# Layer-1 input projections by a seven-product block scheme, with the layer-1 memory keys and values computed in layer 0

## The chip, the cores and the metric

The kernel is one program on all 8 cores of a Trainium2 chip; every core works on 1024 of the 8192 tokens. The metric is the device time of the slowest core, in microseconds (us).

A program on all cores has two states. In the fast one, executions of a kernel agree within about 0.3%. In the slow one, the cores of one die (cores 0 to 3, or 4 to 7), sometimes of both, are granted a lower TensorE clock, and the time is longer. Every run lists span and clock of each core, so the state is known.

The engines are called as the profile calls them: PE (matmul), PEld (weight load), DVE (vector), ACT (scalar), POOL and SP (here they mostly issue transfers).

## The reference, cut to what matters

A decoder trunk of two layers, width 2048. Layer 0 mixes tokens by dilated attention, layer 1 by a gated unit; both also attend to 256 memory tokens; each is followed by a SwiGLU block of width 5632.

```python
def _spatial_gating_mixer(h, w_in, ln_g, ln_b, w_spatial, b_spatial):   # layer 1
    proj = h @ w_in                               # 2048 -> u 1536, v 1536, q_mem 512
    u, v, q_mem = jnp.split(proj, [SGU_W, 2 * SGU_W], axis=-1)
    u = jax.nn.gelu(u)
    v = _layer_norm(jax.nn.gelu(v), ln_g, ln_b)
    v = v.reshape(b, s // SGU_CHUNK, SGU_CHUNK, SGU_GROUPS, SGU_GROUP_DIM)
    ...                                           # w_s: masked lower triangular, 128 x 128 per group
    mixed = jnp.einsum('gts,bnsgc->bntgc', w_s, v) + b_spatial.T[None, None, :, :, None]
    return u * mixed.reshape(b, s, SGU_W), q_mem

def _memory_attention(q_mem, mem_n, w_mem_kv):    # both layers
    kv = mem_n @ w_mem_kv                         # depends on mem and weights only, not on x
    ...
```

Two facts carry the change. `h @ w_in` is a large matrix product, which a two-by-two block scheme (Strassen's, in Winograd's form) computes with seven block products for eight, at the price of sums of blocks. And the memory keys and values of layer 1 do not depend on `x`, so they can be computed at any time.

## The kernel before

The feed-forward blocks of both layers already use the seven-product scheme (`quads` forms the token sums, `tsum` the weight sums, the `prod` calls are the seven products). Layer 1's input projections do not: each output tile is 16 products over the contraction of 2048.

Weights come as 1 MB bf16 or f16 blocks (2 MB of f32 in HBM, cast by the transfer), through a ring of four slots. A load waits until the previous user of its slot is done.

```python
    class Ring:
        order = (96, 104, 112, 120)
        def load(self, src, half=False, at=None):
            if at is None:
                at = self.order[self.n % 4]
                self.n += 1
            ...
            pooldma(lambda g: g.dma_start(out=rb.ap, in_=src), [], [rb.r()], f"w{at}", 2.1)

    # layer 0: values and keys, query/key of head set 0, memory k/v of layer 0, memory queries
    for f in v_ + qk0[0:4] + k_ + qk0[4:8] + mu[0:4] + qk0[8:12] + mu[4:6] + qm_units():
        f()
    ...
    # layer 1 (after the feed-forward of layer 0)
    for th in range(2):
        for m in range(4):
            q_unit(m, th, wq[m // 2])        # memory queries
    l1_mem_b()                               # memory k/v of layer 1: 4 weight blocks
    for th in range(2):
        for m in range(4):
            ...
            mem_attn(1, m, ...)
    l1_tables()
    v_all((0, 1))                            # v, gelu, layer norm per tile
    for pc in range(6):
        u_piece(pc, "u")                     # u, gelu, then the gate of v and the product with u
```

In `v_all` the tokens are the stationary operand (512 weight columns stream past), in `u_piece` and `q_unit` the weights are (512 tokens stream past). An operation line of the profile such as L974 or L1180 is the line of a helper, so one line stands for many operations.

The softmax here doesn't subtract the row's maximum and nothing guards it: scores larger than these inputs give would overflow.

## Time and profile before

| | |
|---|---|
| three runs | 2665.65, 2873.76, 3029.14 us |
| profiled execution | 2664.8 us, clocks 0.987 to 0.989 on all cores |
| PE busy | 96% of the span |
| layer-1 projections and gating | 260 us, of which PE busy 248 |
| four matmul groups there | v 384, u 384, query 128 products of 512 columns; memory k/v 64 of 256 and 32 of 512 |

The head of the profile page gives busy time of each engine, share of the span, and count of instructions; part 4 gives the chain of waits that ended last, by engine.

```profile
PE 2559.5 (96%) x12625; PEld 1209.1 (45%) x12703; DVE 1379.7 (52%) x2321; ACT 721.2 (27%) x1139; POOL 146.5 (5%) x247
PE 86%; DMA 5%; DVE 4%; issue 3%; ACT 2%; POOL 0%; DVEq 0%; ACTq 0%; another core or an unknown queue 0%; SPq 0%; POOLq 0%
```

PE is the limit nearly everywhere. The next view gives, for a stretch of time, its length, the busy time (and instructions) of each engine, the granted PE clock, the busy share of the DMA engines, and GB/s. This is the kernel before; the first two stretches are layer 0's memory weights, the last two layer 1's projections and, inside them, the memory attention.

```profile
core 2: us, PE busy (x) PEld busy (x) DVE busy (x) ACT busy (x) POOL busy (x), PEclk, DMA share, GB/s
306.80:317.20 10.40, 6.62 (x77) 4.94 (x78) 8.48 (x26) 1.77 (x6) 2.12 (x4) 1.00 0.86 127
317.20:357.30 40.10, 39.53 (x212) 20.95 (x215) 20.82 (x42) 6.76 (x13) 2.11 (x4) 1.00 0.94 154
1462.00:1722.00 260.00, 248.14 (x1337) 121.03 (x1339) 107.05 (x225) 81.28 (x125) 10.77 (x20) 1.00 0.47 90
1528.60:1567.00 38.40, 31.96 (x142) 13.46 (x144) 12.04 (x21) 31.85 (x47) 0.00 (x0) 1.00 0.07 21
```

In layer 0 the DMA engines are 0.86 to 0.94 busy. In layer 1 they are half idle. In the memory attention PE idles 6.4 of 38.4 us while ACT is busy 31.9.

The timeline of PE shows how layer 0's memory queries (L747) follow layer 0's memory values (L713) without a gap. Columns: start, length, engine, line, operation, output<-inputs, shape, count.

```profile
353.89 1.89 PE L713 MATMUL psall<-ring_0_137,stg_54 128*128 128x512 bf16 x8
355.62 1.89 PE L713 MATMUL psall<-ring_0_136,stg_54 128*128 128x512 bf16 x8
357.34 1.89 PE L747 MATMUL psall<-hT,ring_0_138 128*128 128x512 bf16 x8
359.07 1.89 PE L713 MATMUL psall<-ring_0_137,stg_54 128*128 128x512 bf16 x7
360.80 10.52 PE L747 MATMUL psall<-hT,ring_0_138 128*128 128x512 bf16 x47
```

Where PE waits in layer 1, longest in total first: total us, times, longest.

```profile
PE psall L1474 <- ACT vtm_a L1480: 2.8, 2, 1.8
PE psall L1426 <- DVE Btab L1430: 1.7, 1, 1.7
PE psall L1538 <- DVE hTq L1044: 1.6, 1, 1.6
PE psall L1501 <- DVE vtm_b L1493: 1.6, 1, 1.6
```

L1474 is v waiting for a gelu (the table of ACT alternates between gelu and exp there), L1501 is the gate waiting for the layer norm.

### The profile page before, as it was taken

To read this page: it belongs to the slowest core of one execution; us is meant where nothing else is said; L and a number is where in the kernel's file an instruction comes from. 1 tells how busy PE (TensorE), PEld (TensorE's weight loads), DVE (VectorE), ACT (ScalarE), POOL (GpSimd) and SP (SyncE) were. 2 spreads that over 40 slices of the span, in tenths; PEclk is the share of its full clock that TensorE was granted. 3 is DMA by queue.
4 is the path that set the end of the run, shared out by engine and by line. 5 is a ranking of instruction groups with operands and counts; after the bars stand their busy time and mean duration, and the time that the engine had idled before them with its cause. 6 is when DMAs were issued, how large, how long until landed. Compare 5 with 4: busy or idle time off the path is not lost.

```text
span 2664.8 us, 34291 instructions; the slowest of 8 cores (2648.5 to 2664.8 us)
## 1 busy us (share of the span) xinstructions
PE 2559.5 (96%) x12625; PEld 1209.1 (45%) x12703; DVE 1379.7 (52%) x2321; ACT 721.2 (27%) x1139; POOL 146.5 (5%) x247
## 2 busy tenths in 40 slices
PE   6999999999999999989999999999999999999998
PEld 2344446554444444444444534445444444444443
DVE  4873536657434343446766425327444434356766
ACT  3532224235323232320002351115322323210003
POOL 2001000000000000000000000000000000000002
PEclk9999999999999999999999999999999999999999
DMA  9745772343565656566662814432656555566654
GB/s 153 105 61 93 127 131 49 64 121 92 109 115 117 116 103 116 101 144 127 141 135 50 166 33 86 88 64 49 130 107 126 106 113 105 111 138 132 137 124 143
DMA packets 91892, 288.30 MB, mean 108 GB/s; under 512 B 6736, under 2 KB 56656, under 8 KB 68304
## 3 DMA queue, kind: packets, MB, share of 16 engines
q0 software_dynamic: 36912, 217.87, 47.0%
q1 hardware_dynamic: 54816, 68.24, 8.0%
q8 instruction: 103, 1.69, 0.3%
q14 instruction: 61, 0.50, 0.1%
HBM read 471.44 MB, written 32.51 MB: 189 GB/s over the span
## 4 chain that ended last, share of the span: by engine, by line
PE 86%; DMA 5%; DVE 4%; issue 3%; ACT 2%; POOL 0%; DVEq 0%; ACTq 0%; another core or an unknown queue 0%; SPq 0%; POOLq 0%
PE psall L1180 38%; PE psall L1327 17%; PE psall L729 6%; PE psall L1561 4%; PE psall L1523 3%; PE psall L684 2%; PE psall L639 2%; PE psall L1474 2%; PE psall L655 2%; PE psall L1073 2%; DMA hid<-fs_74 1%; PE psall L1538 1%; PE psall L747 1%; PE psall L883 1%; PE psall L1038 1%
## 5 line engine op out<-in xcount | busy, mean ns | idle before, releaser
L974 DVE TENSOR_TENSOR xs<-psall,xs 128x512 f32<-128x512 f32 x400 | 269.4, 690 | 233.1 <-PE psall L1327 156.7
L1180 PE MATMUL psall<-hTq,ft_71 128*128 128x512 f16 x704 | 167.9, 382 | 3.7 <-DVE hTq L1063 3.7
L1180 PE MATMUL psall<-hTq,ft_72 128*128 128x512 f16 x704 | 166.3, 379 | 0.0
L1180 PEld LDWEIGHTS psall<-hTq,ft_71 128*128 128x128 f16 x704 | 69.1, 98 | 88.1 <-issue 6.3
L1180 PEld LDWEIGHTS psall<-hTq,ft_72 128*128 128x128 f16 x704 | 68.9, 98 | 83.1
L1180 PE MATMUL psall<-hTq,fr_67 128*128 128x512 f16 x384 | 87.3, 379 | 1.0 <-DVE hTq L1044 1.0
L980 ACT ACTIVATE junkB_127<-xs 128x1024 bf16<-128x1024 f32 x16 | 16.8, 1051 | 246.9 <-DVE xs L974 246.4
L1180 PE MATMUL psall<-Sq_65,ft_71 128*128 128x512 f16 x352 | 83.3, 379 | 0.0
L1180 PE MATMUL psall<-Sq_64,ft_72 128*128 128x512 f16 x352 | 83.2, 379 | 0.0
L1180 PE MATMUL psall<-Sq_65,ft_72 128*128 128x512 f16 x352 | 83.2, 379 | 0.0
L1180 PE MATMUL psall<-Sq_64,ft_71 128*128 128x512 f16 x352 | 83.2, 379 | 0.0
L1180 PE MATMUL psall<-hTq,fr_70 128*128 128x512 f16 x352 | 79.9, 379 | 0.0
L1180 PE MATMUL psall<-hTq,fr_69 128*128 128x512 f16 x352 | 79.7, 379 | 0.0
L1180 PE MATMUL psall<-hTq,fr_68 128*128 128x512 f16 x320 | 72.7, 379 | 0.0
L980 ACT ACTIVATE junkB_126<-xs 128x1024 bf16<-128x1024 f32 x8 | 8.5, 1057 | 234.3 <-DVE xs L974 233.7
L1161 DVE TENSOR_TENSOR ft_71<-fr_67 128x2048 f16<-128x2048 f16 x22 | 26.9, 1225 | 84.3 <-PE psall L1180 83.9
L1161 DVE TENSOR_TENSOR ft_72<-fr_70 128x2048 f16<-128x2048 f16 x20 | 24.5, 1225 | 83.2 <-PE psall L1180 83.2
L1044 DVE TENSOR_TENSOR hTq<-psall,gT_s 128x1024 f16<-128x1024 f16 x48 | 56.9, 1218 | 19.2 <-PE psall L1038 18.8
L1161 DVE TENSOR_TENSOR ft_72<-fr_68 128x2048 f16<-128x2048 f16 x20 | 24.5, 1225 | 81.5 <-PE psall L1180 79.4
L1161 DVE TENSOR_TENSOR ft_71<-fr_69 128x2048 f16<-128x2048 f16 x20 | 24.5, 1225 | 80.8 <-PE psall L1180 80.8
L1186 ACT COPY snap_79<-psall 128x512 f32<-128x512 f32 x59 | 34.6, 586 | 113.8 <-PE psall L1180 113.8
L1186 ACT COPY snap_81<-psall 128x512 f32<-128x512 f32 x59 | 34.6, 586 | 112.9 <-PE psall L1180 112.9
(1321 smaller groups left out, 4762.4 us busy)
## 6 DMA issues: line engine op xcount, KB each, us to landing
fr_67<-wgu POOLq DMA_DIRECT2D x24, 1024.0 KB, 8.6
fr_69<-wgu POOLq DMA_DIRECT2D x22, 1024.0 KB, 8.5
fr_70<-wgu POOLq DMA_DIRECT2D x22, 1024.0 KB, 8.5
fr_68<-wgu POOLq DMA_DIRECT2D x20, 1024.0 KB, 8.6
ring_0_135<-w POOLq DMA_DIRECT2D x8, 1024.0 KB, 9.7
xs<-xo SPq DMA_DIRECT2D x8, 1024.0 KB, 10.4
y<-xs SPq DMA_DIRECT2D x16, 512.0 KB, 4.1
ring_0_136<-w POOLq DMA_DIRECT2D x7, 1024.0 KB, 11.6
```

Of the source, the lines that this page charges most:

```text
L639: pe([(lambda t, k=k, w=w: t.matmul(bank(b), hb[k * n + tt * 128:k * n + tt * 128 + 128], w[(k % 8) * 512:(k % 8 + 1) * 512], start=(k == ...
L655: pe([(lambda t, k=k: t.matmul(bank(b)[:, 0:n], w[k * 256 + c0:k * 256 + c0 + 128], hb[k * n:(k + 1) * n], start=(k == 0), stop=(k == 15)) ...
L684: pe([(lambda t, k=k, hf=hf: t.matmul(bank(b), own_tile(hT[k * TOK:(k + 1) * TOK], gi, j), ws[hf][(k % 8) * 512:(k % 8 + 1) * 512], start= ...
L729: proj(b, 512, [(lambda t, k=k: t.matmul(bank(b), w[k * 256 + c * 128:k * 256 + c * 128 + 128], hT[k * TOK + th * 512:k * TOK + th * 512 + ...
L974: dve(lambda v: v.tensor_tensor(out=xa, in0=bank(b), in1=xa, op=ALU.add), [PB(b), xr], [xr], 512)
L1044: dve(lambda v, b=b, gb=gb, dst=dst: v.tensor_tensor(out=dst, in0=bankb(b).rearrange("p (a c) -> p a c", c=128), in1=gb, op=ALU.mult), [PB ...
L1161: dve(lambda v: v.tensor_tensor(out=T[0:2048], in0=w[1024:3072], in1=w[0:2048], op=ALU.subtract), [w.r(0, 3072)], [T.r(0, 2048)], 2048, 2)
L1180: pe([(lambda t, k=k: t.matmul(bank(b), W[blk * 1024 + k * 128:blk * 1024 + k * 128 + 128], f(k), start=(first and k == 0), stop=(last and ...
L1186: act(lambda a: a.copy(out=s_.ap, in_=bank(b)), [PB(b)], [s_.r()], 512)
L1327: pe([(lambda t, k=k: t.matmul(bank(b), f(u, k), w[k * 512:(k + 1) * 512], start=(first and k == 0), stop=(last and k == hG - 1), skip_gro ...
L1523: proj(b, 512, [(lambda t, k=k, b=b, c=c, th=th, w=w: t.matmul(bank(b), w[k * 256 + c * 128:k * 256 + c * 128 + 128], hTq[hq_(k, th * 512, ...
L1561: pe([(lambda t_, k=k, hh=hh, hf=hf: t_.matmul(bank(b), gTm[(hh * 8 + k) * TOK + t * 128:(hh * 8 + k) * TOK + t * 128 + 128], ws[hh][k * 5 ...
```

## The change

The intent: take 7/8 of the PE work of three projections (v, u, memory queries), keep the products that go into the gate in one buffer (v, then the gated v, then u times it, all in place), and move the layer-1 memory keys and values out of layer 1, whose buffers the new sums need, into layer 0. The core of the diff, with cuts:

```diff
-    memd = nc.dram_tensor("memd", [128, 4096], BF16).ap()
+    mk1d = nc.dram_tensor("mk1d", [128, 1024], F16).ap()
+    mv1d = nc.dram_tensor("mv1d", [128, 1024], BF16).ap()
 ...
-    spdma(lambda q: q.dma_start(out=memd, in_=memT1p.ap), [memT1p.r()], [kreg("memd")], "m1", 1.05)
 ...
-    for f in v_ + qk0[0:4] + k_ + qk0[4:8] + mu[0:4] + qk0[8:12] + mu[4:6] + qm_units():
+    mu1 = mem_units(1, memT1p, mkt, mvt)
+    for f in v_ + qk0[0:4] + k_ + qk0[4:8] + mu[0:4] + qk0[8:12] + mu[4:6] + mu1:
         f()
+    spdma(lambda q: q.dma_start(out=mk1d, in_=mkt.ap), ...)
+    spdma(lambda q: q.dma_start(out=mv1d, in_=mvt.ap), ...)
+    for f in qm_units():
+        f()
 ... layer 1, v: two token tiles and 256 columns to a product, seven products for a block of 4 tiles x 512 columns
+        def f1():
+            prod(X, A(0, 0), "B11", True, False)
+            st["s1"] = snapshot(X)
+        def f2():
+            prod(Y, A(1, 0), "B21", True, True)
+            add(fin(0, 0), two(bank(Y)), [PB(Y)], st["s1"])
+        def f3():
+            prod(X, S(1), "T2", False, False)
+            st["s2"] = snapshot(X)
 ...
+    v_units(0)
+    quads(0)
+    quads(1)
+    sums_v(vu[0][0])
+    v_raw(0)
 ... layer 1, query and u pieces, seven products each; memory attention between them
+    tsum_u(wq0)
+    piece_u(wq0, (12, 13), False)
+    tsum_u(wq1)
+    mem_pair((0, 1))
+    piece_u(wq1, (14, 15), False)
+    ln_all()
+    mem_pair((2, 3))
+    l1_tables()
+    for pc in range(6):
+        for c in range(2):
+            for th in range(2):
+                gate(2 * pc + c, th)
+        tsum_u(wu[pc])
+        piece_u(wu[pc], (2 * pc, 2 * pc + 1), True)
 ...
+            act(lambda a: a.activation(out=u.ap, in_=src, func=AF.Gelu), ..., after=[mem_last[0]])
```

A `snapshot` is a copy of a running partial sum out of PSUM by ACT: the scheme reuses partial sums in several outputs.

## The prediction

> All numbers are for the fast state: the profiled execution (2664.8 us, all clocks 0.987 to 0.989) matches the fastest time (2665.65). 2873.76 and 3029.14 I take for the slow state.
>
> **What bounds it now.** Busy table: PE 96%, DVE 52%, ACT 27%; the chain of waits is 86% PE. By windows, layer-1 projections and gating (1462 to 1722 us) take 260 us with PE busy 248: 12 us idle, 6.4 of it in the memory attention (1528 to 1567), 1.6 before a gate (layer norm). At 306 to 357 us (layer 0's memory weights) the DMA engines are 0.86 to 0.96 busy and PE waits 3.6 us for a weight block: already DMA-bound.
>
> **Removed.** Timeline: eight 128x512 matmuls take 1.726 us (0.216 each), 32 of 128x256 take 3.49 us (0.109 each, own weight load each, so loads stay hidden). Before: v 384, u 384, query 128 of 512 columns = 193.3 us. After: v 672 of 256 columns (73.2), u and query 448 of 512 (96.6) = 169.8. PE saves 23.5 us, all on the chain. The normed memory's store, just ahead of the DMA-bound stretch, goes: about 2 us.
>
> **Added.** DVE: token sums 16 x 0.68, v weight sums 12 x 1.225, u and query weight sums 8 x 2.6: 46 us. ACT: some 56 snapshots of 0.59 = 33 us. Per 12 us piece ACT is busy about 5 us, DVE 9 to 10: hidden, as in the feed-forward, which runs the same scheme without gaps. At the entry (1462 to 1500) DVE is 27.5 of 38 us busy and gets 10 us more before the third product can run, and gelu and exp tables (1.28 us a load) may alternate: I charge 3 us. Layer norm is batched behind the query pieces; gelu is held until memory attention is done, so the gelu/exp swaps there go: 5 us less idle, limited by single accumulator banks.
>
> **Moved.** Layer-1 memory k/v (13.9 us of PE, 1514.7 to 1528.6) goes to layer 0, ahead of the memory queries. PE work is neutral, but its four 1 MB blocks enter, at about 339 us, a queue that delivers one in 7 to 8 us, while each feeds PE 3.5 us. The four-slot ring puts the query block behind them: it lands at 383 to 390 us instead of 355.6, with 14 us of work to cover 26 to 32. Nothing else is ready (later units share PSUM banks in program order). I charge 12 us (8 to 18) of new PE wait. The Trainium skill ("Trainium Kernel Development and Optimization", Key Constraints) says that DMAs of all queues share 16 engines and interleave; landing times growing from 8.5 to 18 us in this stretch agree.
>
> **Sum.** 2665 - 23.5 - 2 + 3 - 5 + 12 = about 2650 us. 8 in 10: 2636 to 2668. Faster by over 2%: 2%; within 2%: 96%; slower by over 2%: 2%.
>
> **What would show it.** 896 matmuls of 512 columns become 448 plus 672 of 256; the stretch from 1462 to 1722 shrinks by 13.9 + 23.5 + a few us; in layer 0, a new DMA-ended wait of 8 to 18 us before the memory-query matmuls, whose end moves from 387 to about 411 to 416 us.
>
> **What would make it wrong.** No wait in layer 0: about 2638. 256-column products over 0.109 us, DVE lateness in v pieces, or memory attention serialised by one accumulator: up to 2670.

## The result, and the profile after

| | before | changed |
|---|---|---|
| runs | 2665.65, 2873.76, 3029.14, 2664.49 us | 2651.20, 2927.68, 2989.39, 2653.95 us |
| state | fast, slow, slow, fast | fast, slow, slow, fast |
| median of all four | 2769.70 | 2790.81 |
| profiled execution (fast) | 2664.8 | 2649.6 |

The ratio of the fast runs is 0.9954 (95% interval 0.993 to 0.9978). A ratio is the mean time of one kernel's fast runs over that of the other's of the same rounds, so it is not quite the ratio of the medians.

The fast runs, 2651.20 and 2653.95, lie in the predicted range, 1 and 4 us from the predicted 2650. The median of all four runs, 2790.81, is the midpoint between a fast and a slow run and lies far above it. Both things are taken up below.

The head of the page and the chain by engine, changed kernel:

```profile
PE 2547.4 (96%) x12927; PEld 1230.0 (46%) x12927; DVE 1424.3 (54%) x2341; ACT 747.5 (28%) x1191; POOL 146.8 (6%) x248
PE 87%; DMA 6%; DVE 3%; issue 2%; ACT 1%; POOL 0%; DVEq 0%; ACTq 0%; POOLq 0%; SPq 0%
```

PE work fell by 12 us; DVE and ACT work rose by 45 and 26 us and mostly hid. DMA's rounded share of the chain went from 5% to 6%; what stands behind it, PE's timeline in layer 0 shows. Changed kernel; L717 and L729 are now memory keys and values, of layer 0 (input `stg`) and then of layer 1 (`memT1p`), L763 the memory queries. The brackets give the idle time before a group and what ended it.

```profile
358.09 1.91 PE L717 MATMUL psall<-memT1p,ring_0_148 128*128 128x256 bf16 x16
359.84 1.89 PE L729 MATMUL psall<-ring_0_147,stg_56 128*128 128x512 bf16 x8
361.57 1.91 PE L717 MATMUL psall<-memT1p,ring_0_148 128*128 128x256 bf16 x16
365.14 3.65 PE L717 MATMUL psall<-memT1p,ring_0_145 128*128 128x256 bf16 x32 [1.66 <-DMA ring_0_145<-wkv]
372.08 6.36 PE L729 MATMUL psall<-ring_0_146,memT1p 128*128 128x512 bf16 x16 [3.29 <-DMA ring_0_146<-wkv]
378.93 3.61 PE L729 MATMUL psall<-ring_0_147,memT1p 128*128 128x512 bf16 x16 [0.49 <-DMA ring_0_147<-wkv]
386.18 13.97 PE L763 MATMUL psall<-hT,ring_0_148 128*128 128x512 bf16 x64 [3.64 <-DMA ring_0_148<-w]
```

Four waits, 9.1 us in all, each ended by a weight block. And one group is slow: at 372.08, 16 products take 6.36 us where the same 16 take 3.61 us at 378.93, since PE ran at half clock then (the clock records of this core have 0.5 from 370.8 us on, for 6.8 us). Queries start at 386.2, not at 357.3.

In layer 1 the changed kernel's waits of PE are others than before:

```profile
PE psall L1718 <- DVE G_93 L1721: 1.9, 5, 0.8
PE psall L1513 <- DVE tV_99 L1485: 1.5, 1, 1.5
PE psall L1767 <- DVE G_93 L1697: 1.4, 1, 1.4
PE psall L1513 <- DVE G_93 L1541: 1.0, 1, 1.0
PE psall L1718 <- DVE Btab L1738: 0.7, 1, 0.7
PE psall L1734 <- DVE Btab L1738: 0.7, 1, 0.7
```

and by stretches (all of layer 1's projections; the memory attention; the first gates):

```profile
core 1: us, PE busy (x) PEld busy (x) DVE busy (x) ACT busy (x) POOL busy (x), PEclk, DMA share, GB/s
1475.00:1709.00 234.00, 225.12 (x1518) 136.23 (x1517) 156.08 (x250) 111.14 (x182) 10.92 (x20) 1.00 0.46 82
1597.00:1640.00 43.00, 43.00 (x201) 19.47 (x200) 18.44 (x29) 24.64 (x45) 1.41 (x2) 1.00 0.32 68
1640.00:1656.00 16.00, 11.93 (x78) 5.72 (x77) 15.18 (x33) 7.30 (x13) 1.06 (x2) 1.00 0.51 89
```

The memory attention, 6.4 us idle before, runs with PE busy 43.00 of 43.00. Right behind it is a new hole: in 16 us of gate tables and first gates PE idles 4.1 us, with DVE busy 15.2 of 16.

To see where time came from, I took marks from the trace of all eight cores (first or last matmul of a stage) and averaged over the cores. In us; positive means that the kernel reaches the mark later than the kernel before.

| mark | changed | control (changed, run again) |
|---|---|---|
| end of layer 0's halo keys | -1.5 | -1.3 |
| end of the memory queries, layer 0 | +25.4 | +25.8 |
| last gate/up product of layer 0 | +24.8 | +24.7 |
| last down product of layer 0 | +20.4 | +21.7 |
| first output-projection product of layer 1 | -13.8 | -12.6 |
| end | -15.9 | -14.2 |

So layer 0 loses 27 us up to the end of the queries, of which 13.9 are the matmuls that moved, and layer 1 wins 34. The down-projection of layer 0 gets 3.0 to 4.4 us shorter. Of this, 2.6 us are the change's too: layer 1's first products already run there, 25 query products of 512 columns before (5.4 us), 26 v products of 256 columns after (2.8 us). The rest differs from run to run. Behind the first output-projection product the changed kernel is 1.6 to 2.1 us shorter; so are all its versions below (1.6 to 3.8), while e2, a version of the kernel before, is not (0.4 longer). Nothing here explains that part.

### The profile page after: what moved, and what is told of

Its sections match the earlier page's. It is cut to its first block, busy times and chain, and to the rows that moved or that the text cites. A ratio compares the mean times of both kernels' runs of the same rounds, so it can differ in the third digit from the quotient of the medians.

```text
span 2649.6 us, 34898 instructions; the slowest of 8 cores (2634.0 to 2649.6 us)
## 1 busy us (share of the span) xinstructions
PE 2547.4 (96%) x12927; PEld 1230.0 (46%) x12927; DVE 1424.3 (54%) x2341; ACT 747.5 (28%) x1191; POOL 146.8 (6%) x248
## 4 chain that ended last, share of the span: by engine, by line
PE 87%; DMA 6%; DVE 3%; issue 2%; ACT 1%; POOL 0%; DVEq 0%; ACTq 0%; POOLq 0%; SPq 0%
PE psall L1210 38%; PE psall L1357 17%; PE psall L745 6%; PE psall L1767 4%; PE psall L1673 3%; PE psall L1513 2%; PE psall L671 2%; PE psall L700 2%; PE psall L655 2%; PE psall L1103 2%; DMA stg_56<-xT 1%; PE psall L763 1%; PE psall L913 1%; DMA ring_0_148<-w 1%; PE psall L1068 1%
## 5 line engine op out<-in xcount | busy, mean ns | idle before, releaser
L1191 DVE TENSOR_TENSOR ft_73<-fr_69 128x2048 f16<-128x2048 f16 x22 | 26.9, 1224 | 85.1 <-PE psall L1210 84.2
## 6 DMA issues: line engine op xcount, KB each, us to landing
fr_69<-wgu POOLq DMA_DIRECT2D x24, 1024.0 KB, 10.2
```

The costliest lines, as they stand in the source:

```text
L1191: dve(lambda v: v.tensor_tensor(out=T[0:2048], in0=w[1024:3072], in1=w[0:2048], op=ALU.subtract), [w.r(0, 3072)], [T.r(0, 2048)], 2048, 2)
```

## The experiments

All times below are of fast runs. "Layer-1 stage" is the time from the last down product of layer 0 to the first output-projection product of layer 1, mean over the eight cores of the profiled execution; it is 233.4 us before, and 199.2 and 199.1 in the two profiles of the changed kernel. Job A ran on one chip, job C on another. In job A the kernel before had one run of 2697.24 us that counts as fast; without it its fast runs average 2667.1. It lowers all four ratios of that job by 0.2%, so I compare times and marks. The differences of 9 us are told from noise because the fast runs of a job hardly overlap (control 2650.8 to 2657.5 us, e1 2642.8 to 2647.3, e3 2642.5 to 2645.7).

| run | job | fast runs of it, mean us | fast ratio to before | end of memory queries and k/v, layer 0 | layer-1 stage against before |
|---|---|---|---|---|---|
| kernel before | A, C | 2667.1, 2666.2 | | 0 | 0 |
| control (changed) | A | 2653.1 | 0.9929 | +25.8 | -34.3 |
| e1 no loads | A | 2644.6 | 0.9897 | +15.4 | -34.1 |
| e2 before with loads | A | 2683.1 | 1.0041 | +18.3 | +1.2 |
| e3 between | A | 2644.2 | 0.9895 | +14.3 | -34.1 |
| e4b gates later | C | 2654.7 | 0.9957 | +24.9 | -33.7 |
| e5b both | C | 2644.2 | 0.9917 | +13.6 | -33.8 |
| e6b v by eight | C | 2657.4 | 0.9967 | +25.2 | -29.5 |
| e7b u by eight | C | 2665.9 | 0.9999 | +25.0 | -21.8 |

(In e3 and e5b the memory values come last, not the queries; the figure is the end of whichever is last.)

**Theory.** The products save what their count says; half of that is lost in layer 0, because four more weight blocks stand in the queue ahead of the query weights. **Rival 1**: the loss in layer 0 lies in the moved matmuls themselves, their PSUM banks and evictions, not in the loads. **Rival 2**: the sum of bytes counts, not the order. **Rival 3**: the seven-product pieces fall short of their count, since snapshots, sums and merges hold them up.

### Control: the changed kernel again

> The changed kernel once more, unedited, as a control on the chip of the next runs. Expected: about 0.995 of the kernel before (2651 to 2655 us where that takes 2665), on fast runs, and the same stage lengths as in the first profile: about 25 us later than before at the end of the memory queries, about 34 us shorter from the end of layer 0 to the output projection of layer 1. Rival (the small gain is noise of the run): the two stages differ from the first profile by more than a few us.

Measured: 2653.1 us, marks within 1.7 us of the first profile (table above). The gain of 14 us over 2667.1 and its two parts are real and repeat.

### e1: the same matmuls without the loads

```diff
-    mu1 = mem_units(1, memT1p, mkt, mvt)
+    mu1 = mem_units(1, memT1p, mkt, mvt, reuse=True)   # reads the two blocks of layer 0's memory values
```

> Layer-1 memory k/v in layer 0 keeps its 96 matmuls but reads the two weight blocks of layer 0's memory values, which are already there: the four extra loads are gone, and the result is wrong on purpose. My theory (a queue of weight loads, one block in 7 to 8 us, is what PE waits for): the end of the memory queries moves from 25 us later than before to about 14 us later (the matmuls alone), and the time falls by 9 to 13 us, to about 0.991 of before. Rival (the wait is in the matmuls' own PSUM banks, evictions or order, not in the loads): nothing changes, 0.995.

Measured: the result is wrong (relative error 0.06). 2644.6 us, 8.5 less than the control; the end of the queries comes 15.4 us later than before, where layer 0's halo keys already end 1.5 later: the 13.9 us of the matmuls and nothing more. The stretch of 60 us that holds memory k/v and queries, first the kernel before, then changed, then e1 (each under its own column line):

```profile
core 2: us, PE busy (x) PEld busy (x) DVE busy (x) ACT busy (x) POOL busy (x), PEclk, DMA share, GB/s
355.00:415.00 60.00, 59.68 (x278) 27.46 (x283) 20.00 (x37) 26.71 (x50) 2.77 (x6) 1.00 0.56 94
```

```profile
core 1: us, PE busy (x) PEld busy (x) DVE busy (x) ACT busy (x) POOL busy (x), PEclk, DMA share, GB/s
355.00:415.00 60.00, 50.92 (x254) 25.02 (x252) 4.35 (x8) 9.37 (x18) 4.72 (x9) 0.94 0.87 149
```

```profile
core 0: us, PE busy (x) PEld busy (x) DVE busy (x) ACT busy (x) POOL busy (x), PEclk, DMA share, GB/s
355.00:415.00 60.00, 59.69 (x305) 30.31 (x310) 10.18 (x20) 17.80 (x35) 2.64 (x5) 1.00 0.52 99
```

With the loads PE idles 9 us and is granted 0.94 of its clock, at a DMA share of 0.87; without them it is busy throughout at full clock, at 0.52. Rival 1 falls.

### e2: the kernel before, with the loads and nothing else

```diff
-    ... + mu[4:6] + qm_units():
+    ... + mu[4:6] + [lambda i=i: R.load(wkv[4 + i]) for i in range(4)] + qm_units():
```

> The kernel before, plus only the four extra weight loads of layer-1 memory k/v at the same place in the ring of layer 0; nothing reads them, so the result stays right. My theory: the loads alone delay the memory queries by as much as the changed kernel does, since the matmuls there hide under the loads: end of the memory queries 22 to 28 us later, time 1.008 to 1.011 of before (2687 to 2694 us). Rival (the matmuls are what costs): no delay, or only a few us, 1.000.

Measured: 2683.1 us, 16 more than before; the queries end 18.3 us later and layer 0's attention 15.6 us later. The direction is as expected, so four loads that nobody reads cost more than the whole change saves. The size is under the range that I had written (22 to 28; 2687 to 2694). The timeline of the POOL queue gives the likely reason: with no matmul holding the slots, it issued the first query block ahead of the last two idle blocks (at 357.94, against 360.88 and 362.60), so two blocks fewer stood before it than in the changed kernel; it landed at 373.1 us, there at 385.8. The wait itself:

```profile
356.71 5.34 PE L713 MATMUL psall<-ring,stg 128*128 128x512 bf16 x24
373.34 16.08 PE L747 MATMUL psall<-hT,ring 128*128 128x512 bf16 x64 [11.28 <-DMA ring<-w]
```

After 11.3 us of waiting, the 64 products take 16.08 us where they take 13.97 in the changed kernel: the half clock again, 2.1 us.

### e3: the memory blocks between the query blocks

```diff
-    qmT = sb("qmT", 160 * KB, 8 * KB)
+    qmT = sb("qmT", 168 * KB, 8 * KB)
-    for f in ... + mu[4:6] + mu1:
-        f()
-    ...
-    for f in qm_units():
+    for f in ... + mu[4:6]:
+        f()
+    qm = qm_units()
+    for f in qm[0:4] + mu1[0:4]:
+        f()
+    ...                                  # store the keys
+    for f in qm[4:8] + mu1[4:6]:
         f()
-    for m in range(4):
+    for m in (2, 0, 3, 1):               # so that no head overwrites queries still to be read
```

> The changed kernel with the same four loads and the same matmuls, but ordered query block 0, memory keys, query block 1, memory values, so that each query block (14 us of PE work for one load) covers two memory blocks; the memory-query buffer moves by 8 KB and the heads are taken in another order to make room. My theory (order of the queue): almost all of the wait goes; end of the memory queries and memory k/v about 15 us later than before instead of 25, time 8 to 12 us less than the changed kernel, about 0.991 of before. Rival (the total of bytes in this stretch sets the time, whatever the order): no change, 0.995.

Measured: correct, 2644.2 us, 9 us less than the control and 23 less than the kernel before; attention of layer 0 ends 14.4 us later than before, where the changed kernel is 26.0 later. PE in the same 60 us, with the DMA engines busier than ever:

```profile
core 1: us, PE busy (x) PEld busy (x) DVE busy (x) ACT busy (x) POOL busy (x), PEclk, DMA share, GB/s
355.00:415.00 60.00, 60.00 (x311) 30.25 (x310) 10.93 (x21) 17.25 (x33) 4.75 (x9) 1.00 0.92 158
```

The same bytes, the same matmuls, and no wait: rival 2 falls. A query block feeds PE 13.8 us for one load, a memory block 3.5 us; alternated, the work of one pays for the wait of the other. This version beats both kernels.

### e4: the first gates behind the first products

```diff
+    tsum_u(wu[0])
+    P.prio += 12                # tables and first gates rank behind the piece's first products
     l1_tables()
     for pc in range(6):
         ...
+        if pc == 0:
+            P.prio -= 12 + 24
```

> The changed kernel, with only the order of work changed where the first gated piece begins: the gate tables and the first four gates come behind that piece's first three products instead of ahead of them. In the changed kernel's trace PE waits there for the vector engine in small pieces, some 4.5 us in all between 1643 and 1655 us. My theory: these waits are order, not throughput, and go: stretch from the end of layer 0 to the output projection 3 to 5 us shorter than in the control (about 2648 us in all). Rival (the vector engine is the limit of the whole gated stage): the waits move to a later piece, no change.

This job (B) met a chip on which all 46 runs, of the kernel before and of four others, took over 3000 us.

> The same kernel as in the run before it, which met a chip that gave the slow state in every run. Expectation unchanged: stretch from the end of layer 0 to the output projection of layer 1 3 to 5 us shorter than in the control, about 2648 us in the fast state. Rival: the waits move to a later piece, no change.

Measured: 2654.7 us; layer-1 stage 33.7 us shorter than before, the control 34.3. No gain: the expected 3 to 5 us did not come. But the edit did not do what it was meant to do. PE at the start of this place, first in the changed kernel (core 1), then in e4b (core 3); L1734 makes the tables, L1718 the gates:

```profile
1640.56 0.38 PE L1734 MATMUL psall<-wsT,onesh 128*128 128x512 f16 x1
1640.78 1.89 PE L1673 MATMUL psall<-hTq,ring_1_196 128*128 128x512 f16 x8
1644.73 0.38 PE L1718 MATMUL psall<-wsT,G_93 128*128 128x128 f16 x4 [0.66 <-DVE Btab L1738]
```

```profile
1645.73 0.38 PE L1734 MATMUL psall<-wsT,onesh 128*128 128x512 f16 x1
1645.94 1.89 PE L1673 MATMUL psall<-hTq,ring 128*128 128x512 f16 x8
1649.90 0.38 PE L1718 MATMUL psall<-wsT,G 128*128 128x128 f16 x4 [0.66 <-DVE Btab L1738]
```

The 5.2 us between them are the two cores' own: counted from the end of the last down product, the first table begins at 133.15 us in the changed kernel and 133.13 in e4b, the first gate at 137.32 and 137.30. Tables and first three gates stayed where they were; only from the fourth gate on the order of PE differs. In the same 16 us counted from that mark, PE idles 4.1 us in the changed kernel and 3.4 in e4b. So e4 does not decide between order and throughput. What speaks for the rival is the DVE timeline: in both kernels DVE works through this place almost without a pause (15.2 and 15.3 of these 16 us), with the gate tables (12 small operations, 3.2 us) first and the gates and merges behind them. That another order would not help is argued, not shown. Building the tables earlier was not tried: their buffer is the ring slot of the query weights until then.

### e5: both orders together

> Both orders together: memory blocks between the query blocks in layer 0, and the first gates behind the first products in layer 1. Expected: the gains add, 11 to 16 us less than the changed kernel's 2652 (2637 to 2642 us), all of it in these two stages. Rival: a gain in one stage is given back at the next wait for loads, and the sum is less than 9 us.

Job B too, slow in every run. Again:

> Again, for the same reason. Expectation unchanged: the gains of the two orders add, 2637 to 2642 us in the fast state, 11 to 16 us less than the control. Rival: less than 9 us, as one gain is given back.

Measured: 2644.2 us in two fast runs, 22 us less than the kernel before in the same job, about as e3 alone (23; the control 14). The expectation of a sum failed, as the edit of e4 adds nothing; the gain of e3 is there once more, on another chip.

### e6: v by eight products

The units of v are replaced by 16 products of 512 columns per tile and a gelu straight from PSUM, as in the kernel before; the token sums for u come behind them.

```diff
-    v_units(0); quads(0); quads(1); sums_v(vu[0][0]); v_raw(0); ...
+    for cb in range(3):
+        for t in (...):
+            b = nextbank((0, 1, 2, 3, 4, 5))
+            for hf in range(2):
+                pe([... 8 products of 512 columns ...], ...)
+            act(gelu from bank(b)); dve(bn_stats)
+            if cb == 2 and t >= 4:
+                quads(t - 4)
```

> The changed kernel with v computed by eight products of 512 columns as in the kernel before; u, query and all else as changed. By matmul counts PE gets 384 x 0.2157 = 82.8 us in place of 672 x 0.109 = 73.2 us, 9.6 us more. At the entry of layer 1 nothing then waits for weight or token sums, where I charged 3 us: theory, the stage gets 6 to 8 us longer than in the control (2658 to 2660 us). Rival (256-column products run no faster in sum than the eight of 512, because weight loads show): no change or shorter.

> Again, for the same reason. Expectation unchanged: v by eight products makes the layer-1 stage 6 to 8 us longer than in the control (2658 to 2660 us in the fast state). Rival: no change or shorter.

The first of the two fell into job B. Measured in the second: 2657.4 us, in the direction expected. The layer-1 stage is 4.8 us longer than in the control, less than the 6 to 8 that I had written; and 0.9 of it is the mark's, since fewer v products run ahead of it (9 of 512 columns, 26 of 256 in the control). So the seven products of v, at 256 columns, are worth about 4 us net. The count of products says 9.6 us; of that, 3.5 us comes back in idle time (8.6 us of PE gaps in this stage in the changed kernel, 5.1 in e6b, summed over the trace, mean of the cores), most of it the entry, for which I had charged 3 us, and 1.7 us in small late starts (see below).

### e7: u and memory queries by eight products

`piece_u` makes four outputs of 16 products each, without weight sums and snapshots; four subtractions give back the token block that the sums of v had overwritten.

> The changed kernel with u and query pieces by eight products, without weight sums and snapshots; v stays with seven, and the one token block that its sums overwrote is restored by four subtractions. By matmul counts PE gets 512 x 0.2157 = 110.4 us in place of 448 x 0.2157 = 96.6 us. Theory: the layer-1 stage gets 13 to 16 us longer than in the control (2665 to 2668 us), since the seven-product pieces run without gaps. Rival (snapshots, sums and merges on the other two engines cost part of it): under 10 us.

> Again, for the same reason. Expectation unchanged: u and query by eight products make the layer-1 stage 13 to 16 us longer than in the control (2665 to 2668 us in the fast state). Rival: under 10 us.

Measured in the second (the first was in job B): 2665.9 us, the time of the kernel before (2666.2). The layer-1 stage is 12.5 us longer than in the control, against 13.8 by count and the 13 to 16 expected: just under the range, well over the rival's 10. So u and queries return nine tenths of their count. Rival 3 is true for v (more than half of the count is lost), hardly for u.

## Why the prediction was right or wrong

**The time.** The step that failed is the first one: "All numbers are for the fast state" and "2873.76 and 3029.14 I take for the slow state". The reading of the states was right, and 2651.20 and 2653.95 are in the range. But the forecast took the fast state for the time to come: it gave one narrow range for one state, when two of the three times in front of me were slow; the median over the four runs of the changed kernel, two fast and two slow, is 2790.81 and lies outside, as the median of the kernel before (2769.70) lies 105 us above its own fast runs. What the runs showed in its place: half of the executions were slow, at 2927.68 and 2989.39 us. The slow state is not the change's doing. In the changed kernel's run of 2927.68 us the four cores of die 0 took 2900.9 to 2926.1 us at clocks of 0.877 to 0.884; the four of die 1 took 2640.0 to 2654.7 us at 0.986 to 0.988, as in a fast run. In job B the kernel before took 3007 us and more in all its 11 runs. A slow and a fast execution compared, core 4, in 400 us of layer 0's feed-forward and after; first of the e4 kernel in job B, then of the changed kernel:

```profile
core 4: us, PE busy (x) PEld busy (x) DVE busy (x) ACT busy (x) POOL busy (x), PEclk, DMA share, GB/s
1000.00:1400.00 400.00, 400.00 (x1526) 165.66 (x1524) 159.84 (x258) 84.91 (x143) 15.84 (x30) 0.81 0.51 100
```

```profile
core 4: us, PE busy (x) PEld busy (x) DVE busy (x) ACT busy (x) POOL busy (x), PEclk, DMA share, GB/s
1000.00:1400.00 400.00, 397.52 (x1841) 179.68 (x1840) 223.66 (x362) 66.06 (x111) 18.58 (x35) 1.00 0.61 124
```

PE is busy all the time in both and does 1526 products in the one, 1841 in the other: 0.83, with a granted clock of 0.81. In the records of that slow execution core 4 was granted 0.8125 for 2211 of its 3006 us; none of the eight cores of a fast profile of before or of the changed kernel shows that value at all. 0.8125 is 13/16, and the Trainium skill ("TensorE: Matmul & The Clock Gate", "Seeing it yourself") has a limiter with just this ratio, of peak current, for a whole die. That it is this limiter is an inference from the same number; no run here changes the current, and what brings a chip into the slow state stays open.

**Seven products for eight.** Right in mechanism, too large in size. Predicted 23.5 us; taken back separately, v is worth about 4 us (e6b) and u with the queries 12.5 us (e7b), some 16 us net of what they add. The 256-column products do run at 0.109 us: in the changed kernel groups of eight follow each other in 0.87 us. The difference to 23.5 is idle time at the entry and the first gates, and late starts: in this stage some 25 groups begin about 0.12 us late behind a semaphore, 3.1 us in all (one group before, 11 in e6b), which the profile counts as busy. I had assumed "without gaps".

**The store of the memory.** Predicted 2 us; not shown. The mark before the DMA-bound stretch is 1.3 to 1.5 us earlier in the changed kernel, but over all runs without this store it lies between 1.5 us earlier and 1.5 us later (e1), and in e2, which keeps the store, 0.4 us earlier.

**Layer 0's wait.** Right, shown by e1 and e3, and supported by e2. Predicted 12 us (8 to 18), queries' block at 383 to 390 us, their end at 411 to 416. In the trace the block lands at 385.8, the queries start at 386.2 and end at 413.8. Blocks landed somewhat closer together than I had assumed: every 6.6 us on average from 344 to 410 us, for my 7 to 8. (All these loads are issued by POOL, so that their landing times grow shows a full queue; it does not test how queues of several engines share the DMA engines.) The stage is 26.9 to 27.1 us longer than before, 13 more than the matmuls; 9.5 of these are idle time (12.9 against 3.4 us between the halo keys and the end of the attention, summed over the trace), the rest PE at half clock after the waits, which I had not put in.

**Layer 1's idle time.** Predicted 3 us more at the entry and 5 less by the end of the table swaps. The entry is as predicted (1.5 and 1.0 us of waits for the sums, and 3.5 us gone in e6b). The memory attention and the layer norm now cost no wait, 8 us less than before. But 4.1 us of wait are new, at the first gates, where DVE is busy 15.2 of 16 us. I had averaged DVE over a piece ("9 to 10 of 12 us") and not looked at the start, where tables, gates and merges fall together. Net: 11.4 us of gaps before, 8.6 after.

**The sum.** 15.5 us predicted (2665 to 2650), 14.2 and 15.9 measured as means of the cores, 14 us in the control's fast runs. Part of this agreement is luck. By the prediction's terms layer 0 loses 23.9 us (13.9 + 12 - 2) and layer 1 gains 39.4 (13.9 + 23.5 - 3 + 5). Measured are 25.4 to 25.8 lost and about 36.8 gained (34.2 in the stage and 2.6 ahead of its mark), 11 us in all. The other 3 to 5 us lie in stages for which the prediction has no term, 1.6 to 2.1 of them behind the first output projection. The mechanisms hold, but two terms were missing (the first gates, the half clock), the products were put too high, and unpredicted gains made up for it.

## What to carry to other kernels

Work that depends on nothing can be moved anywhere on PE, but its weights come along, and a place is free only if the loads are: count, for each block, the PE time that it feeds against the time that it takes to arrive, and alternate rich blocks with poor ones (e3: 9 us from order alone). Judge an engine's room where work starts, not as the average over a piece. After an edit of the order, check in the trace, counted from a common mark, that the order changed (in e4 it hardly did).

## What the Trainium skill lacked or had wrong

- "TensorE: Matmul & The Clock Gate", "Back-to-back issue gap", gives 131 ns per product of 512 columns and 81 ns per product of 128 columns as the sustained rate in a stream with weight loads. The runs show 216 ns at 512 (eight in 1.73 us), 109 ns at 256 and 56 ns at 128 (eight in 0.45 us), each with its own weight load. The formula that the page calls isolated, N/2.4 + 2.5 ns, is the one that holds.
- The same page, "Seeing it yourself", has a die go to 13/16 clock once three of its cores run dense products, and says to budget 1.95 GHz for all-core work. In fast executions all eight cores ran dense at full clock (mean 0.983 to 0.992 in the fast runs of jobs A and C but one, and no record of 0.8125 in the fast profiles). The value appears in slow executions only, and which state comes depends on chip and time: 46 of 46 runs over 3000 us on one chip, most runs fast on two others. The page lacks that both happen.
- The same page, "What's actually happening", has half clock after at least one idle window of about 3.4 us. The records do have stretches of 3.4, 6.8, 10.2 or 13.7 us at 0.5, but the window need not be idle: in the profiles of before, changed, control and e2, past the first 200 us and up to the last 100, PE was busy for up to 0.47 of the 3.4 us ahead of a drop (216 drops), and no 3.4 us window with PE busy for less than 0.36 kept full clock. What a drop costs here: 2.7 us for 16 products after a wait of 3.3 us, 2.1 us for 64 after 11.3 us.
- "ScalarE: Activation LUTs", "What ACT_TABLE_LOAD costs", has 1283 ns for the load, which the trace shows exactly, and 1380 ns of drain beside it. In the trace of the kernel before the load starts 0.02 us after the previous operation ends and the next starts 0.01 us after it, so a switch costs 1.3 us there; no drain is seen.
- No page gives the rate of a casting load with all cores at work. Here 1 MB bf16 blocks out of 2 MB f32 arrived every 6.6 us on average when the queue was full, and took 7.8 to 8.7 us from issue to landing when alone.
